# Opening of a two-layer decoder: two product tiles in one fixed order with the transposes, four k tiles apart

## The chip, the cores and the metric

The kernel runs on one core of a Trainium2 chip. The metric is the device time of one execution in microseconds (us), the median over several runs. The engines are TensorE (PE, matrix products and transposes), VectorE (DVE), ScalarE (ACT), GpSimd (POOL) and SyncE (SP). DMAs are issued from SP's queue and from ACT's; an issue on ACT's queue stands in the order of ACT's own work.

## What is computed

Two layers of a decoder with four parallel mixer branches, for 1024 prompt positions and 8 decoding rows. Each layer begins with a norm and one combined projection:

```
h = rms_norm(x, norm_g)
(a_b, a_c, a_h, a_gate, s_q, s_k, s_v, s_gate,
 c_u, c_v, c_gate, d_q, d_k, d_v, d_gate) = jnp.split(h @ w_in, SPLIT_POINTS, axis=-1)
z = a_c * a_h                                    # A: gated depthwise convolution of width 3
q = rope(s_q, pos); k = rope(s_k, pos); v = s_v  # B: sliding-window attention with sinks
vn = layer_norm(c_v, v_ln_g, v_ln_b)             # C: gating over chunks of 128 positions
dq = rope(d_q, pos); dk = rope(d_k, pos); dv = d_v   # D: three dilated attentions, joined by softmax
branches = stack([y_a * silu(a_gate), y_b * silu(s_gate), y_c * silu(c_gate), y_d * silu(d_gate)])
merged = sum(sigmoid(h @ w_merge) * (branches @ w_branch))
x = x + merged @ w_out
```

A last norm follows the second layer; caches and states are outputs too.

## The kernel before

**Layout.** The activations lie transposed: x^T in 8 k tiles of 128 rows by 1032 columns (8 decoding rows, then 1024 positions). Columns are taken in three chunks of 344 for the products and in three groups of 392, 384 and 256 for the start (`GROUPS`). Each fp32 product is made of three matmuls on a high and a low part (`mm_cols`, lines L178, L181, L182: h x wh, l x wh, h x wl). The parts of the weights come from ACT (hi, L154) and POOL (lo, L156), those of x^T from ACT (hi, L207) and DVE (lo, L209); for every fourth k tile ACT makes a scaled copy and POOL the low part (L213, L214). The norm's factor of a position, rtok, is applied to the results, so that products can start before the norm is known.

**The start (L251 to L272).** The input rows (xs: the decoding rows, xin: blocks of 128 positions) are loaded, 72 PE transposes (L259 for the 8 rows, L262 for a block) turn them into x^T by group and k tile, DVE copies each result from PSUM to xT (L264), and `split_x` makes both parts from that copy. Eight DMAs on ACT's queue store xT for the residual (L267), and nine squares on ACT (L272) sum up the squared rows.

**Then in each layer.** `rope_products` makes the key tile kB and the first query tile qB0, chunk by chunk, with ACT evicting each accumulator (L281). ACT's root (L325) and DVE's reciprocal (L326) give rtok. For the rotary factors rtok is spread over the partitions: DVE builds diagonal matrices dg (L332), PE multiplies them with ones (L333), ACT, DVE and POOL apply the result rr (L336 to L338). `rope` turns kB and qB0 (its shifted copies qs are DMAs on ACT's queue, L290). `tm_v` makes V for the window branch and the dilated branch, in blocks of 128 positions by 256 columns through `tm_group` (products L372, L375, L376; ACT evicts a block with its rtok at L391 and stores it at L393). A second query tile qB1 and then the gating branch's v, 384 columns wide, by the same lines L372 to L376, follow.

**Order.** Each engine runs its instructions in the order of its own queue. A scheduler sets that order from the program and from estimated times; `keep_in_program_order` pins an instruction to the place where it is written, and `issue_after` keeps everything issued inside it behind a given instruction. PSUM accumulators come from three pools: psA (three of one bank, `pacc`), psM (three of one bank, `pmisc`) and psS (one of two banks, `pscore`). A raw weight tile has two buffers, the split parts have four each.

**Further on.** The spatial weights wsp are loaded (L460) and transposed by PE (L465). `Decode.scores` transposes the decode queries on PE (L656). For the dilated groups (L890, L891, L906, L907) decode scores are issued ahead of a group's attention.

Of the kernel before, what the change touches and what calls it, by code (L numbers as in the profile page):

```python
# [7 lines left out]
F32 = mybir.dt.float32  # L8
F32R = mybir.dt.float32r
# [23 lines left out]
def kernel(ctx: ExitStack, tc: tile.TileContext, i, o, c):  # L33
# [65 lines left out]
    sp.dma_start(ident, c["ident"])  # L99
# [48 lines left out]

    def split_w(shape, dmas):
# [4 lines left out]
        act.activation(hi, raw, AF.Copy)  # L154
# [12 lines left out]
    def w_pair(l, c0, j):  # L167
# [4 lines left out]
        return r  # L172

# [30 lines left out]
    def split_x(l, k, cs, x, h, on_dve=True):  # L204

        g, hi, lo = gcol[:, l, k:k + 1], h[0][k][:, cs], h[1][k][:, cs]
        act.activation(hi, x, AF.Identity, scale=g)  # L207
        if on_dve:
            dve.scalar_tensor_tensor(lo, x, g, hi.bitcast(F32), op0=ALU.mult, op1=ALU.subtract)  # L209
# [22 lines left out]

    xs = slot("xs")[:NS, :DM]
    for q in range(2):
        fs = slice(q * DM // 2, (q + 1) * DM // 2)
        for n in range(3):
# [3 lines left out]
            if q == 0 and n == 0:  # L240
                sp.dma_start(xs, i["x_sample"].rearrange("b s d -> (b s) d"))
                sp.dma_start(gcol, i["norm_g"].rearrange("l (k p) -> p l k", p=P))
    w_first = [w_std(win_cols(0, S_K, P), KT)]
# [24 lines left out]
    sq0 = sm.tile([P, 9], F32, tag="sq0", name="sq0")  # L268
    junk = slot("junk")
    for n in range(9):  # L270
        src, M = (xin[n], P) if n < 8 else (xs, NS)
        act.activation(junk[:M, :DM], src[:M, :DM], AF.Square, accum_out=sq0[:M, n:n + 1])  # L272

    for l in range(2):
# [35 lines left out]
        w2 = w_first if l == 0 else [w_std(win_cols(l, S_K, P), KT)]  # L310
        w2.append(w_pair(l, S_Q, 0))
        kq = rope_products(w2, [slot("kB"), slot("qB0")])
# [14 lines left out]
        for n0, n1 in ((8, 9), (0, 4), (4, 8)):  # L327
            ps = pmisc()
            M = NS if n0 == 8 else P
            for n in range(n0, n1):  # L330
# [815 lines left out]
```

## Time and profile before

| | us |
|---|---|
| median of 3 runs | 2382.03 |
| lowest, highest | 2381.37, 2385.53 |
| profiled execution | 2387.34 |
| its span on the core | 2385.6 |
| PE busy within it | 2365.5 |
| DVE, ACT, POOL busy | 895.2, 687.4, 843.5 |

The times of single instructions come from the profiled execution. In its rows a line such as L178 is a line of the kernel above, `out<-in` are tile names, and xN joins N like instructions in a row; two instructions of an engine overlap by a part of their durations, so the distance between two starts is what one costs the engine. In the tables by windows PEclk is TensorE's granted clock as a share of its upper level (2.4 GHz; 0.50 is 1.2 GHz).

### The profile page before, as it was taken

The page shows a single profiled execution, that of the slowest core. Times are in us where ns is not written, and L with a number is a line of the kernel's source. Part 1 is how long each engine was busy: PE and PEld are TensorE (multiplying, and loading weights), DVE is VectorE, ACT ScalarE, POOL GpSimd, SP SyncE. Part 2 cuts the span into 40 slices and gives each one's busy share as a digit, 9 for nine tenths or more (in the row PEclk, how much of TensorE's full clock was granted, in tenths as well). Part 3 has the DMA queues.
Part 4 walks back from the last instruction along what each step waited for, and adds up shares of the span by engine and source line. Part 5 has one row for each costly group of instructions (what it writes and reads, how often), then busy time and mean ns, then how long its engine had stood idle before and what let it go on. Part 6 is the DMA issues. An engine that isn't in the chain of part 4 may idle for free.

```text
span 2385.6 us, 38754 instructions
## 1 busy us (share of the span) xinstructions
PE 2365.5 (99%) x15896; PEld 2305.1 (97%) x15896; DVE 895.2 (38%) x1938; ACT 687.4 (29%) x1522; POOL 843.5 (35%) x556
## 2 busy tenths in 40 slices
PE   7999999999999999999999999999999999999999
PEld 6999999999999999999999999999999999999999
DVE  4345466335312222324333455554452221213143
ACT  5133432223212222223322244323231221212243
POOL 3333234432223444434442322353322233444330
PEclk9999999999899999999999999999989999999999
DMA  7342423433322212224542423244442122222232
GB/s 237 98 123 79 119 69 109 132 102 106 100 71 88 77 55 97 64 70 123 150 146 72 145 72 98 69 151 113 111 126 67 58 91 66 98 67 62 75 99 101
DMA packets 295962, 235.82 MB, mean 99 GB/s; under 512 B 52756, under 2 KB 279696, under 8 KB 293416
## 3 DMA queue, kind: packets, MB, share of 16 engines
q1 hardware_dynamic: 267952, 206.25, 28.8%
q10 hardware_dynamic: 27832, 27.10, 4.1%
q8 instruction: 124, 2.03, 0.4%
q14 instruction: 54, 0.44, 0.1%
HBM read 192.35 MB, written 76.47 MB: 113 GB/s over the span
## 4 chain that ended last, share of the span: by engine, by line
PE 98%; DVE 1%; DMA 0%; ACT 0%; SPq 0%; issue 0%; ACTq 0%; DVEq 0%
PE acc L181 27%; PE acc L182 27%; PE acc L178 27%; PE acc L372 2%; PE acc L375 2%; PE acc L376 2%; PE sc L540 2%; PE ms L569 2%; PE ms L558 1%; PE ms L733 1%; PE ms L479 0%; PE ms L1042 0%; DMA wr<-in_w_in_dram 0%; DVE xT L264 0%; DVE h0l L209 0%; PE ms L333 0%
## 5 line engine op out<-in xcount | busy, mean ns | idle before, releaser
L156 POOL TENSOR_TENSOR wl<-wr,wh 128x384 fp32r<-128x384 f32 (+2 forms) x228 | 476.9, 2093 | 827.3 <-ACT wh L154 698.7
L181 PE MATMUL acc<-h1l,wh 128*128 128x344 f32 x1584 | 511.5, 323 | 0.0
L182 PE MATMUL acc<-h0h,wl 128*128 128x344 f32 x1584 | 510.4, 323 | 0.0
L178 PE MATMUL acc<-h0h,wh 128*128 128x344 f32 x1584 | 509.3, 322 | 0.9 <-DVE xT L264 0.9
L178 PE MATMUL acc<-h1h,wh 128*128 128x344 f32 x1584 | 510.2, 322 | 0.0
L182 PE MATMUL acc<-h1h,wl 128*128 128x344 f32 x1584 | 509.5, 322 | 0.0
L181 PE MATMUL acc<-h0l,wh 128*128 128x344 f32 x1584 | 508.9, 321 | 0.0
L154 ACT ACTIVATE wh<-wr 128x384 fp32r<-128x384 f32 (+2 forms) x228 | 205.2, 901 | 421.4 <-PE acc L181 393.6
L1005 DVE TENSOR_TENSOR th<-acc,rr 128x344 f32<-128x344 f32 x192 | 99.1, 516 | 553.5 <-PE acc L182 553.5
L181 PEld LDWEIGHTS acc<-h1l,wh 128*128 128x128 f32 x1584 | 299.9, 189 | 4.2 <-issue 3.6
L181 PEld LDWEIGHTS acc<-h0l,wh 128*128 128x128 f32 x1584 | 299.2, 189 | 3.9 <-issue 3.5
L182 PEld LDWEIGHTS acc<-h1h,wl 128*128 128x128 f32 x1584 | 299.7, 189 | 2.8 <-issue 2.3
L178 PEld LDWEIGHTS acc<-h0h,wh 128*128 128x128 f32 x1584 | 299.1, 189 | 2.8 <-issue 1.2
L182 PEld LDWEIGHTS acc<-h0h,wl 128*128 128x128 f32 x1584 | 298.6, 189 | 2.9 <-issue 2.3
L178 PEld LDWEIGHTS acc<-h1h,wh 128*128 128x128 f32 x1584 | 299.6, 189 | 1.4 <-issue 1.0
L1011 POOL TENSOR_TENSOR mg<-mg,th 128x344 f32<-128x344 f32 x144 | 134.0, 931 | 303.3 <-DVE th L1010 303.3
L1006 ACT ACTIVATE th<-th 128x344 f32<-128x344 f32 x192 | 94.3, 491 | 496.9 <-DVE th L1005 496.4
L178 PE MATMUL acc<-yh,wh 128*128 128x344 f32 x576 | 184.4, 321 | 0.0
L182 PE MATMUL acc<-yh,wl 128*128 128x344 f32 x576 | 184.3, 320 | 0.0
L181 PE MATMUL acc<-yl,wh 128*128 128x344 f32 x576 | 184.1, 320 | 0.0
L181 PE MATMUL acc<-ml,wh 128*128 128x344 f32 (+3 forms) x384 | 123.2, 321 | 0.0
L182 PE MATMUL acc<-mh,wl 128*128 128x344 f32 (+3 forms) x384 | 123.0, 321 | 0.0
(278 smaller groups left out, 3256.6 us busy)
## 6 DMA issues: line engine op xcount, KB each, us to landing
wr<-in_w_merge_dram SPq DMA_DIRECT2D x64, 512.0 KB
out_dram<-in_cache_dil_kv_dram SPq DMA_DIRECT2D x128, 255.9 KB
wr<-in_w_in_dram SPq DMA_DIRECT2D x60, 512.0 KB
y<-yscr SPq DMA_DIRECT2D x18, 516.0 KB
wr<-in_w_branch_dram SPq DMA_DIRECT2D x48, 192.0 KB
wr<-in_w_in_dram SPq DMA_DIRECT2D x32, 256.0 KB
wr<-in_w_out_dram SPq DMA_DIRECT2D x16, 512.0 KB
out_dram<-in_cache_dil_kv_dram SPq DMA_DIRECT2D x16, 511.0 KB
```

Of the source, the lines that this page charges most:

```text
L154: act.activation(hi, raw, AF.Copy)
L156: pool.tensor_tensor(lo, raw, hi.bitcast(F32), op=ALU.subtract)
L178: mm = pe.matmul(ps[:, :n], hi[:, k], xh[k][:, cs], start=(k == 0), stop=False)
L181: pe.matmul(ps[:, :n], hi[:, k], xl[k][:, cs], start=False, stop=False)
L182: pe.matmul(ps[:, :n], lo[:, k], xh[k][:, cs], start=False, stop=(k == kt - 1))
L372: mm = pe.matmul(ps[:M, :N], lh, hi[:, k % kk], start=(k == 0), stop=False)
L375: pe.matmul(ps[:M, :N], ll, hi[:, k % kk], start=False, stop=False)
L376: pe.matmul(ps[:M, :N], lh, lo[:, k % kk], start=False, stop=(k == KT - 1))
L540: pin(pe.matmul(ps[:, h, a * 256:a * 256 + u.nk], u.qs[h], u.ks[h], start=True, stop=True))
L1005: dve.tensor_tensor(t, pg[:, :CH], rr[:, cs], op=ALU.mult)
L1006: act.activation(t, t, AF.Tanh, scale=0.5)
L1011: pool.tensor_tensor(mg[m][:, cs], mg[m][:, cs], t, op=ALU.add)
```

## The change

- **Loads.** `ident`, `xs` and `gcol` are loaded from ACT's queue instead of SP's. The first two weight tiles are loaded in halves of four k tiles, between the halves of the input.
- **Dummy products.** 26 matmuls of a matrix of ones with itself into a bank nobody reads (`busy`): 18 at the start, 4 behind each of the first two turns.
- **Turns.** One k tile of one group is a turn. Its transposes go to psM, hi and lo are made from PSUM, lo always on DVE; xT is copied by ACT for even k and by DVE for odd k. Everything is pinned in the order written.
- **Two tiles in step.** Turns run two ahead of the first tile's products, and the second tile's products of a k tile come `LAG = 4` steps behind the first's. The accumulators of chunks 0 and 2 are both halves of psS's one tile, those of chunk 1 come from psA. Halves of weights are split at steps 0, 2, 3 and 6, squares stand at steps 7, 9, 12, 14, 17, 19 and behind the loop, the weights for the first V group are split at steps 18 and 22.
- **Behind the last eviction** of the opening, `issue_after` holds the stores of xT, the root for rtok and the first V group's evictions.
- **In both layers** the rr block and `rope` of kB and qB0 stand behind the first V group, the rr products, the transposes of wsp and of decode queries are pinned, wsp is loaded earlier, and the attention of the first two dilated groups is written ahead of their decode scores.

The diff, cut to its core:

```diff
     ident = cp.tile([P, P], F32, name="ident")
-    sp.dma_start(ident, c["ident"])
+    act.dma_start(ident, c["ident"])
...
+    idle = pacc()
+
+    def busy(n):
+        for _ in range(n):
+            in_order(pe.matmul(idle[:, :P], onesm, onesm, start=True, stop=True))
...
+                act.dma_start(xs, i["x_sample"].rearrange("b s d -> (b s) d"))
+                act.dma_start(gcol, i["norm_g"].rearrange("l (k p) -> p l k", p=P))
+        load_first(0, q)
+    for q in range(2):
+        load_first(1, q)
...
-    for n0, n1 in GROUPS:
+
+    def turn(n0, n1, k):
+
         off = NS if n0 == 0 else 0
         cs = slice(NS + n0 * P - off, NS + n1 * P)
         w = cs.stop - cs.start
-        for k in range(KT):
-            ks_ = slice(k * P, (k + 1) * P)
-            ps = pmisc() if k % 2 else pacc()
-            if off:
-                pe.transpose(ps[:, 0:NS], xs[:, ks_], ident[:NS, :NS])
-            for n in range(n0, n1):
-                c0 = off + (n - n0) * P
-                pe.transpose(ps[:, c0:c0 + P], xin[n][:, ks_], ident)
-            xt = xT0[k][:, cs]
-            dve.tensor_copy(xt, ps[:, :w])
-            split_x(0, k, cs, xt, (hh, hl), k % 4 != 1)
+        ks_ = slice(k * P, (k + 1) * P)
+        ps = pmisc()
+        if off:
+            in_order(pe.transpose(ps[:, 0:NS], xs[:, ks_], ident[:NS, :NS]))
+        for n in range(n0, n1):
+            c0 = off + (n - n0) * P
+            in_order(pe.transpose(ps[:, c0:c0 + P], xin[n][:, ks_], ident))
+        xt = xT0[k][:, cs]
+        if k % 2:
+            in_order(dve.tensor_copy(xt, ps[:, :w]))
+        split_x(0, k, cs, ps[:, :w], (hh, hl))
+        if k % 2 == 0:
+            in_order(act.activation(xt, ps[:, :w], AF.Copy))
...
+    def split_first(a, q):
+        ks_ = slice(4 * q, 4 * q + 4)
+        raw = w_first[a][:, ks_]
+        hi, lo = [t[:, ks_] for t in wf[a]]
+        in_order(act.activation(hi, raw, AF.Copy))
+        pool.tensor_tensor(lo, raw, hi.bitcast(F32), op=ALU.subtract)
+
+    accs = []
+
+    def first_products(a, s):
+
+        c, k = s // KT, s % KT
+        if k == 0 and a == 0:
+            if c == 1:
+                accs.append([pacc(), pacc()])
+            else:
+                two = pscore()
+                accs.append([two[:, 0], two[:, 1]])
+        ps, cs = accs[c][a][:, :CH], slice(c * CH, (c + 1) * CH)
+        hi, lo = [t[:, k] for t in wf[a]]
+        mm = in_order(pe.matmul(ps, hi, hh[k][:, cs], start=(k == 0), stop=False))
+        if s == 0:
+            mark(mm)
+        in_order(pe.matmul(ps, hi, hl[k][:, cs], start=False, stop=False))
+        in_order(pe.matmul(ps, lo, hh[k][:, cs], start=False, stop=(k == KT - 1)))
+        if k == KT - 1:
+            done.append(lambda: in_order(act.activation(kq0[a][:, cs], ps, AF.Copy)))
...
+    LAG = 4
+    squares = (7, 9, 12, 14, 17, 19)
+    for s in range(3 * KT + LAG):
+        if s == 0:
+            for t in turns[:2]:
+                turn(*t[0], t[1])
+                busy(4)
+            split_first(0, 0)
+        if s in (2, 3, 6):
+            split_first(*{2: (0, 1), 3: (1, 0), 6: (1, 1)}[s])
+        if s + 2 < len(turns):
+            turn(*turns[s + 2][0], turns[s + 2][1])
+        while done:
+            done.pop(0)()
+        if s in (18, 22):
+            w_v.append(tm_weights(0, V_FIRST, 4, 4 * len(w_v)))
+        if s in squares:
+            square(squares.index(s))
+        if s < 3 * KT:
+            first_products(0, s)
+        if s >= LAG:
+            first_products(1, s - LAG)
+    for n in range(6, 9):
+        square(n)
+    while done:
+        last = done.pop(0)()
+    opening[0] = False
+    behind_opening = ExitStack()
+    behind_opening.enter_context(tc.issue_after(last.ins))
     for k in range(KT):
         act.dma_start(xres[0][k], xT0[k])
...
+        if l == 0:
+            kq = kq0
+        else:
+            kq = rope_products([w_std(win_cols(l, S_K, P), KT), w_pair(l, S_Q, 0)], [slot("kB"), slot("qB0")])
...
+        tm_v(V_FIRST, 0, w_v if l == 0 else None)
+        behind_opening.close()
+
+        for n0, n1 in ((8, 9), (0, 4), (4, 8)):
+            ps = pmisc()
+            M = NS if n0 == 8 else P
+            for n in range(n0, n1):
+                dg = sm.tile([P, P], F32, tag="dg", name="dg", bufs=2)
+                dve.tensor_scalar(dg[:M, :M], ident[:M, :M], rtok[:M, n:n + 1], None, op0=ALU.mult)
+                tc.keep_in_program_order(pe.matmul(ps[:, (n - n0) * P:(n - n0) * P + M], onesm[:M], dg[:M, :M],
+                                                   start=True, stop=True))
...
         kB, qB = rope(kq[0]), [rope(kq[1])]
-        tm_v([(S_V, P), (D_V, P)], 0)
...
-                pe.transpose(ps[:, g * P:(g + 1) * P], wsp[:, g0 + g], ident)
+                tc.keep_in_program_order(pe.transpose(ps[:, g * P:(g + 1) * P], wsp[:, g0 + g], ident))
...
-                pe.transpose(ps[:NS, :P], q, ident)
+                tc.keep_in_program_order(pe.transpose(ps[:NS, :P], q, ident))
...
+        attention()
         decD.scores(0, dqs[0], dks[0])
-        attention()
...
```

**First place: PE, step 8 of the opening.** Here the second tile's product of k = 4 in chunk 0 (accumulator `sc`, input h0h_135) stands. Before, the first products stood behind all transposes of the first two groups:

```order
L262 MATMUL ms<-ident,xin_120 128x128
L262 MATMUL ms<-ident,xin_122 128x128
L178 MATMUL acc<-h0h_128,wh 128x344
L181 MATMUL acc<-h0l_136,wh 128x344
L182 MATMUL acc<-h0h_128,wl 128x344
L178 MATMUL acc<-h0h_129,wh 128x344
L181 MATMUL acc<-h0l_137,wh 128x344
L182 MATMUL acc<-h0h_129,wl 128x344
```

Now, with what each waits for:

```order
L302 MATMUL ms<-ident,xin_117 128x128 [waits PE_49]
L302 MATMUL ms<-ident,xin_119 128x128
L302 MATMUL ms<-ident,xin_121 128x128
L345 MATMUL acc<-h0h_131,wh 128x344 [waits Activation_49]
L348 MATMUL acc<-h0l_139,wh 128x344 [waits DVE_49]
L349 MATMUL acc<-h0h_131,wl 128x344
L345 MATMUL sc<-h0h_135,wh 128x344 [waits Activation_49]
L348 MATMUL sc<-h0l_143,wh 128x344
L349 MATMUL sc<-h0h_135,wl 128x344 [waits Pool_49]
```

A turn's transposes, the first tile's product of chunk 1 (`acc`) and the second tile's of chunk 0 (`sc`) now alternate; the last of these waits for ACT.

**Second place: ACT, from the kB eviction to the V evictions.** Before, the table load and the root stood ahead of the last evictions, and the stores of xT far ahead:

```order
L272 ACTIVATE junk,sq_340<-xs 8x1024
L325 ACT_TABLE_LOAD
L325 ACTIVATE rtok<-sq_340,epst 128x8
L154 ACTIVATE wh<-wr 128x1024
L281 ACTIVATE kB<-acc 128x344
L325 ACTIVATE rtok<-sq_340,epst 8x1
L154 ACTIVATE wh<-wr 128x768
L281 ACTIVATE qB_359<-acc 128x344
L336 ACTIVATE rr<-ms 128x8
```

Now, with the waits:

```order
L162 ACTIVATE wh<-wr 128x768 [waits DMAHW5_49,PE_49,Pool_49]
L351 ACTIVATE qB_176<-sc 128x344 [waits PE_49]
L383 DMA xres_94<-xT_0_147 128x1032
L383 DMA xres_94<-xT_1_148 128x1032
L383 DMA xres_94<-xT_2_149 128x1032 [waits DMAHW1_49]
L383 DMA xres_94<-xT_3_150 128x1032 [waits DMAHW2_49]
L383 DMA xres_94<-xT_4_151 128x1032
L383 DMA xres_94<-xT_5_152 128x1032
L383 DMA xres_94<-xT_6_153 128x1032 [waits DMAHW6_49]
L383 DMA xres_94<-xT_7_154 128x1032 [waits DMAHW7_49]
L437 ACT_TABLE_LOAD
L437 ACTIVATE rtok<-sq_155,epst 128x8
```

Eight issues of stores, the table load and the root now stand behind the last eviction; three V evictions (L483) follow them.

**Third place: PE, the first dilated group.** Before, the decode query's transpose (dqs) stood with the transposes of the convolution's state and ahead of attention transposes (s):

```order
L780 MATMUL ms<-ident,stt 128x16
L781 MATMUL ms<-ident,z 8x128
L782 MATMUL ms<-ident,z 2x128
L656 MATMUL ms<-ident,dqs_3172 8x128
L558 MATMUL ms<-ident,s 128x128 x4
```

Now:

```order
L201 MATMUL acc<-h0l_144,wh 128x344
L202 MATMUL acc<-h0h_136,wl 128x344
L676 MATMUL ms<-pt,v_3397 64x128 x8
L763 MATMUL ms<-ident,dqs_3190 8x128
L198 MATMUL acc<-h0h_137,wh 128x344
```

It now stands behind the group's products with V (L676).

## Rows read from the trace of the kernel before

**Rows 1.** Page, busy time: engine, busy us, share of the span, instructions.

```profile
PE 2365.5 (99%) x15896; PEld 2305.1 (97%) x15896; DVE 895.2 (38%) x1938; ACT 687.4 (29%) x1522; POOL 843.5 (35%) x556
```

**Rows 2.** Waits of PE: line, what for, us in total, times, longest.

```profile
PE acc L259 <- DMA xs<-in_x_sample_dram: 4.8, 1, 4.8
PE ms L333 <- DVE dg L332: 3.8, 3, 1.5
```

**Rows 3.** Windows: length, busy of PE, PEld, DVE, ACT, POOL, PEclk, DMA share, GB/s.

```profile
0.00:25.00 25.00, 15.63 (x66) 11.13 (x66) 12.27 (x23) 11.08 (x19) 6.00 (x13) 0.86 0.88 243
...
50.00:75.00 25.00, 22.16 (x173) 21.92 (x172) 10.51 (x16) 6.43 (x15) 9.92 (x6) 0.93 0.43 122
```

**Rows 4.** Timeline of PE: start, us, engine, line, operation, [idle before <-releaser].

```profile
27.23 0.40 PE L178 MATMUL acc<-h0h,wh 128*128 128x344 f32 x1 [0.94 <-DVE xT L264]
...
50.42 0.28 PE L372 MATMUL acc<-wh,h0h 128*128 128x256 f32 x1
50.54 0.28 PE L375 MATMUL acc<-wh,h0l 128*128 128x256 f32 x1
...
53.62 0.36 PE L333 MATMUL ms<-dg,onesm 8*128 8x8 f32 x2 [1.39 <-DVE dg L332]
55.44 0.46 PE L333 MATMUL ms<-dg,onesm 128*128 128x128 f32 x2 [1.45 <-DVE dg L332]
...
93.99 0.34 PE L372 MATMUL acc<-wh,h0h 128*128 128x384 f32 x1
```

**Rows 5.** Timeline of ACT and of its DMA queue (ACTq), same columns.

```profile
9.48 0.62 ACT L207 ACTIVATE h0h<-xT,gcol 128x392 fp32r<-128x392 f32 x1 [1.87 <-DVE xT L264]
...
22.34 2.12 ACT L207 ACTIVATE h0h<-xT,gcol 128x384 fp32r<-128x384 f32 x4
...
24.45 0.35 ACTq L267 DMA_DIRECT2D xres<-xT  x1
...
28.98 1.99 ACT L207 ACTIVATE h0h<-xT,gcol 128x256 fp32r<-128x256 f32 x4
...
38.28 0.44 ACT L281 ACTIVATE kB<-acc 128x344 f32<-128x344 f32 x1
38.62 1.05 ACT L272 ACTIVATE junk<-xin 128x1024 f32<-128x1024 f32 x1
...
48.41 1.28 ACT L325 ACT_TABLE_LOAD   x1
49.71 0.30 ACT L325 ACTIVATE rtok<-sq,epst 128x8 f32<-128x8 f32 x1
...
51.38 0.83 ACT L154 ACTIVATE wh<-wr 128x768 fp32r<-128x768 f32 x1
...
54.10 2.54 ACTq L290 DMA_DIRECT2D qs<-kB  x4
...
65.23 0.47 ACT L391 ACTIVATE vn<-acc,rtok 128x256 f32<-128x256 f32 x1 [0.92 <-PE acc L376]
65.73 4.70 ACTq L393 DMA_DIRECT2D vscr<-vn  x1
```

**Rows 6.** Timeline of DVE.

```profile
8.88 0.57 DVE L264 COPY xT<-acc 128x392 f32<-128x392 f32 x1 [7.92 <-PE acc L262]
10.13 0.63 DVE L209 SCALAR_TENSOR_TENSOR h0l<-xT,gcol,h0h 128x392 fp32r<-128x392 f32 x1 [0.69 <-ACT h0h L207]
...
50.04 0.20 DVE L326 RECIPROCAL rtok<-rtok 128x8 f32<-128x8 f32 x1 [12.01 <-ACT rtok L325]
```

**Rows 7.** Timeline of POOL.

```profile
13.78 2.34 POOL L156 TENSOR_TENSOR wl<-wr,wh 128x1024 fp32r<-128x1024 f32 x1 [0.22 <-ACT wh L154]
```

**Rows 8.** Timeline of PE, transposes of the spatial weights, at full clock.

```profile
169.34 0.82 PE L465 MATMUL ms<-ident,wsp 128*128 128x128 f32 x6
```

**Rows 9.** Timeline of PE in layer 1.

```profile
1234.32 0.49 PE L333 MATMUL ms<-dg,onesm 128*128 128x128 f32 x2 [0.91 <-DVE dg L332]
```

**Rows 10.** Timeline of DVE at the first dilated group.

```profile
339.81 2.59 DVE L795 SCALAR_TENSOR_TENSOR yA<-s,cw,yA 128x8 f32<-128x8 f32 x2
```

More of the change, by code (lines that the diff above doesn't have):

```diff
@@ L172, in w_pair, with tm_weights @@
         return r
+    def tm_weights(l, srcs, kk, k0):
+        dmas, c0 = [], 0
+        for col, n in srcs:
+            src = i["w_in"][l, k0 * P:(k0 + kk) * P, col:col + n].rearrange("(k p) m -> p k m", p=P)
+            dmas.append((lambda t, c0=c0, n=n: t[:, :, c0:c0 + n], src))
+            c0 += n
+        r = split_w([P, kk, c0], dmas)
+        copy_piece()
+        return r
+    V_FIRST = [(S_V, P), (D_V, P)]
     def mm_cols(ps, w, kt, xh, xl, cs, first):
@@ L231, in load_x, with load_first @@
             xin.append(xb)
+    idle = pacc()
+    def busy(n):
+        for _ in range(n):
+            in_order(pe.matmul(idle[:, :P], onesm, onesm, start=True, stop=True))
     xs = slot("xs")[:NS, :DM]
+    w_first = [wp.tile([P, KT, P], F32, tag="wr", name="wr", bufs=2) for _ in range(2)]
+    def load_first(t, q):
+        ks_ = slice(4 * q, 4 * q + 4)
+        if t == 0:
+            sp.dma_start(w_first[0][:, ks_], win_cols(0, S_K, P)[:, ks_])
+            return
+        for h in range(2):
+            sp.dma_start(w_first[1][:, ks_, h * 64:(h + 1) * 64], win_cols(0, S_Q + 192 * h, 64)[:, ks_])
     for q in range(2):
@@ new lines, in turn @@
+        ps = pmisc()
[10 more added lines that the diff above has]
+            in_order(act.activation(xt, ps[:, :w], AF.Copy))
+    sq0 = sm.tile([P, 9], F32, tag="sq0", name="sq0")
@@ new lines, with square @@
+    junk = slot("junk")
+    def square(n):
+        src, M = (xin[n], P) if n < 8 else (xs, NS)
+        return in_order(act.activation(junk[:M, :DM], src[:M, :DM], AF.Square, accum_out=sq0[:M, n:n + 1]))
+    busy(18)
+    kq0 = [slot("kB"), slot("qB0")]
+    turns = [(g, k) for g in GROUPS for k in range(KT)]
+    wf = [[wp.tile([P, KT, P], F32R, tag=t, name=t, bufs=4) for t in ("wh", "wl")] for _ in range(2)]
+    w_v = []
+    done = []
+    def split_first(a, q):
+        ks_ = slice(4 * q, 4 * q + 4)
+        raw = w_first[a][:, ks_]
+        hi, lo = [t[:, ks_] for t in wf[a]]
+        in_order(act.activation(hi, raw, AF.Copy))
+        pool.tensor_tensor(lo, raw, hi.bitcast(F32), op=ALU.subtract)
@@ L326 @@
             dve.reciprocal(rtok[:M, ps_], rtok[:M, ps_])
[L327 to L330, printed above, removed]
-                dg = sm.tile([P, P], F32, tag="dg", name="dg", bufs=2)
-                dve.tensor_scalar(dg[:M, :M], ident[:M, :M], rtok[:M, n:n + 1], None, op0=ALU.mult)
-                pe.matmul(ps[:, (n - n0) * P:(n - n0) * P + M], onesm[:M], dg[:M, :M], start=True, stop=True)
-            cs = slice(0, NS) if n0 == 8 else slice(NS + n0 * P, NS + n1 * P)
-            w = cs.stop - cs.start
-            act.activation(rr[:, cs], ps[:, :w], AF.Copy)
-            dve.tensor_tensor(cosT[:, cs], cosT[:, cs], rr[:, cs], op=ALU.mult)
-            pool.tensor_tensor(sinT[:, cs], sinT[:, cs], rr[:, cs], op=ALU.mult)
         cw = sm.tile([P, 3, 3], F32, tag="cw", name="cw")
@@ L443 @@
         bsps = [lngb[:, 6 * P:7 * P], lngb[:, 7 * P:8 * P], wsps[:, 6 * P:7 * P]]
+        load(wsp, i["w_spatial"][l].rearrange("g t s -> t g s"), 2)
         for h in range(2):
@@ L905 @@
         rows()
+        attention()
         decD.scores(1, dqs[1], dks[1])
-        attention()
         out_a(1)
```

45 lines of the change are left out of this document (17 added, 28 removed).

## The prediction

> **What bounds the kernel now.** I read the page's engine table first. TensorE (PE) is busy 99% of the span [rows 1], so an edit pays only by what it takes out of PE's idle time, out of a stretch at half clock, or out of PE's own work. The waits of PE come next [rows 2]: 4.8 us at the start for the sample rows' load, which no edit here removes; 3.8 us in three waits for the diagonal matrices that DVE builds at L332. The table by windows says where it lies [rows 3]: PE is busy 15.63 of the first 25 us, and 22.16 of those from 50 to 75 at a mean granted clock of 0.93, which is 0.07 x 25 = 1.75 us lost to stretches at the lower level (1.2 GHz). From 75 on PE is full, so everything is decided before the first 384-column product of the third group (L372) at 93.99. I call this instant the milestone; what moves it moves the end.
>
> The timeline of PE gives four stations [rows 4]: first product at 27.23, last key/query product just before 50.42, where the V products begin, waits of 1.39 and 1.45 us for L332, and the milestone at 93.99. The 144 products of the first two tiles and the few transposes among them take 23.19 us, so one product costs 0.158, that is 22.75 for all. A 256-column V product costs 0.118 (50.42 to 50.54). From 50.42 to 93.99 are 43.57 us; less both waits and the clock's 1.75 it is 38.98 of steady work.
>
> **The start of the products.** Product 0 now needs one turn instead of all transposes. Before, the first copy of x^T began at 8.88 and the first hi at 9.48 [rows 5, 6]; hi now reads PSUM without that copy, so I start it at S = 8.5 (8 to 9.5). Behind it stand a half split of the weights (0.83 for 768 columns, so an estimate of 0.55 for 512, [rows 5]) and, for the third matmul, POOL's half (2.34 / 2 = 1.2, [rows 7]): the first product is near 9.8 and flows from about 11, 16 us earlier. The dummy products fill time in which PE has nothing else. Their kind is that of L333, of which two took 0.46 [rows 4], so at most 0.23 each, twice that at half clock: 18 of them are 4 to 8 us, about as long as x takes to land, and the other eight 0 to 1.8 us beside the hi that PE waits for. I take 0 and let S reach 9.5.
>
> That is no gain of 16 us, since the transposes now lie among the products. 64 of the 72 do. Six warm transposes in a row took 0.82 [rows 8], so 0.12 each by that row once the last one's tail is taken off: 64 x 0.12 = 7.7. Each turn is also a chain through ACT and DVE.
>
> **ACT's chain, pair by pair.** DVE's lo begins 0.65 after its hi and takes 0.63 (9.48, 10.13, [rows 5, 6]). The order of ACT puts the copy of the even k tile behind that lo, and the next hi behind DVE's copy (0.57): 0.65 + 0.63 + 0.57 + 0.05 of hand-over = 1.90, and 0.53 for that hi (four took 2.12) is 2.43 a pair. For the last group, of 256 columns, hi is 0.50 (four took 1.99), and the pair shrinks by the width to about 1.93. Twelve pairs are 8 x 2.43 + 4 x 1.93 = 27.2; up to the last pair's first hi 25.2. Into this order are put: four half splits (4 x 0.55 = 2.2), six squares (6 x 1.1 = 6.6, by 1.05 and the read of the sum behind it), three evictions (3 x 0.38 = 1.1, by 0.44 less the overlap), one split of V weights (1.05, like a square of the same 1024 columns) [rows 5]. Sum 25.2 + 2.2 + 6.6 + 1.1 + 1.05 = 36.1. So ACT reaches the last pair at 8.5 + 36.1 = 44.6 if PE never holds it up.
>
> PE does. The chunk 0 accumulators of both tiles are one tile now, so the second tile's product of k = 4 waits until the first tile's accumulator has been evicted. PE's own order and ACT's (the first two places shown with the diff) put that eviction behind a split, two hi, a copy, a square, another hi and its copy. From hi of k = 7 on that is 0.53 + 0.53 + 2.43 + 1.05 + 1.28 + 0.44 = 6.3 on ACT, while PE has 9 products and 3 transposes (1.8) and one hi-lo latency (1.28): a hole of about 3 us, in which ACT later waits for the next turn's transposes. With POOL's lo, waited for twice, I put 3 us of PE's making into the chain (0 to 6): 47.6. Then lo (0.5) and what PE still has: in order 23 key/query products (3.6) and 54 V products (6.4). **Last key/query product: 47.6 + 0.5 + 10.0 = 58.1** against 50.42 before, but with 58 of the V products (6.8) done ahead of it.
>
> **From there to the milestone.** PE has 14 V products left (1.65 us), then the fourth V block needs the accumulator of the first, which needs rtok. ACT's order behind the last product is: a 768 split whose buffer that product frees (0.83), the eviction (0.35), eight issues of the x^T stores (8 x 0.35 = 2.8), the table load (1.28), the root (0.30, and the same for the decoding rows' root, beside which DVE's reciprocal runs, 0.20), the V eviction (0.47) [rows 5, 6]: 6.4 us, less 1.65 of cover, a stall of 4.8. Before, the stores' issues lay between hi's in the open stretch, and the load was covered by products. Behind such a stall the clock has fallen before (1.75). Milestone: 58.1 + (38.98 - 6.84) + 4.8 + 1.75 = 96.8, which is **+2.8 us** on 93.99. The 1.39 and 1.45 waits for L332 are gone, this stall stands in their place.
>
> The Trainium skill, page "ScalarE: Activation LUTs", section "What ACT_TABLE_LOAD costs", speaks against putting the load on this path: it counts 1.28 us and a drain of 1.38, 2.66 for a switch. By that the stall would be 6.2 and the time 1.4 later. The row agrees with the 1.28 and not with the drain: the load ran 48.41 to 49.69 and the root began at 49.71 [rows 5]. I stay with the row.
>
> **Later edits.** In layer 1 the dg products stand behind the V group, so PE's wait of 0.91 there [rows 9] should go: -0.9. The spatial weights' load goes earlier and its transposes are pinned: cover is the full PE around them, nothing. The rotary sums with their eight issues on ACT's queue (four took 2.54, [rows 5]) stand behind V's evictions instead of ahead of them; who reads their result comes after the second query tile's 72 products (11.4), so nothing. Decode transposes pinned, and the first two dilated groups' attention ahead of decode scores (the third place shown with the diff): one q transpose moves some 40 rows, so 24 products (3.8 us) that stood between the scores and their masks no longer do, while DVE may stand 2.59 us in L795 behind POOL [rows 10]. Between no loss and 1.5 us a layer; I take +0.6 for both, near the low end, since the products around it can still be put ahead. Sum: 2.8 - 0.9 + 0.6 = **+2.5**.
>
> The profiled execution (2387.34) lies 5.3 above the median of its kernel; its stages are used as differences, so the forecast is 2382.03 + 2.5 = 2384.5.
>
> **The rivals.**
> *PE sets the pace (faster).* If ACT keeps up, because turns run two ahead, the stream is PE's sum: 11 + 22.75 + 6.84 + 7.7 + 1 = 49.3, the milestone 49.3 + 32.1 + 4.8 + 1.75 = 88.0, with the 0.9 of layer 1 -6.9: 2375. With the eviction's hole of 3 us left in, 2378. For it: ACT's sum has 12 x 0.65 of mere waiting for DVE. Against: the order forces that wait. Without the stall at the fourth block and its half clock as well, 2369 (the least likely).
> *The queue of ACT blocks at the stores (slower).* Four of the eight issues wait for an earlier DMA, and all of ACT's work behind them waits too, above all the root. Before, an issue on ACT's queue stood 4.70 us in such a wait (65.73, [rows 5]). One such wait here is +4.7: 2389. The cover of 1.65 is used up already, so a wait adds in full, and from 2.3 us on it decides (2.5 + 2.3 = 4.8). Against: by 59 us the loads of the start have long landed.
> *The attention's order costs in both layers (slower).* +1.5 twice instead of 0.6: 2387.
> *It does not do what it says.* The pinned order holds by construction; but the gain is only moved: transposes into the stream, V products ahead, waits of 2.84 for one of 4.8. That is my forecast.
>
> **How the numbers follow.** About 0.2% (4.8 us) is what a measurement can tell from no change: 2377.3 to 2386.8. My sum, with 0 to 6 us for PE's holds and 8 to 9.5 for S, gives 2381 to 2388: chance 0.47, most of it within the bound. PE's pace 0.27, of which 0.05 ends within the bound (2378). Blocked stores 0.15, attention 0.11, half of it within the bound. Faster 0.24, same 0.48, slower 0.28. The range reaches to 2374 for PE's pace and to 2391 for a blocked issue on top of my sum's upper half; below and above lie 0.1 each.
>
> **What would show it.** The first product near 10 to 11; PE's waits list naming ACT's kB eviction with about 3 us near 25; the last 344-column product of the first group near 58 with V products among the last ones; the fourth V block waiting 4 to 6 us for ACT's V eviction, and half clock behind it; the milestone at 96 to 98; no wait for L332 in either layer. I am wrong if the first products run without holes (PE's pace), if ACT's hi follow one another closer than 2.4 us a pair, or if the milestone is right and the end is not, which puts the error on the attention.

## The result, and the profile of the changed kernel

The changed kernel takes 2411.93 us (median of 4, 2410.96 to 2415.04) against 2383.78 for the kernel before, measured beside it: a ratio of 1.0111 (95% interval 1.0095 to 1.0128), 28 us slower. The forecast was +2.5 and its range ended at 2391. Line numbers below are those of the changed kernel: L227 and L229 make hi and lo, L329 and L330 split the first weights, L345, L348 and L349 are the products of the first two tiles, L351 evicts them, L383 stores xT, L437 is the root, L464, L467 and L468 are the V products, L483 their eviction. In the waits s are the attention's scores, wsT the masked spatial weights, qB the second query tile, vcs the decoding rows' V, qr a decoding query, dqp the rotated query of a dilated group.

The page's table of engines, which answers to [rows 1] (busy us, share of the span, instructions):

```profile
span 2413.3 us, 38855 instructions
PE 2377.1 (99%) x15948; PEld 2315.3 (96%) x15948; DVE 901.7 (37%) x1932; ACT 690.4 (29%) x1530; POOL 844.6 (35%) x552
```

PE's idle time is 2413.3 - 2377.1 = 36.2 us instead of 20.1, and its busy time is 11.6 longer. The first entries of PE's list of waits (total, times, longest; [rows 2] is that of before):

```profile
PE acc L464 <- ACT vn L483: 9.5, 1, 9.5
PE ms L665 <- ACT s L697: 3.7, 2, 1.8
PE sc L345 <- ACT wh L329: 3.4, 1, 3.4
PE ms L586 <- POOL wsT L574: 3.3, 1, 3.3
PE acc L464 <- ACT qB L392: 3.1, 1, 3.1
PE sc L345 <- ACT kB L351: 2.7, 1, 2.7
PE ms L774 <- DVE qr L765: 2.0, 3, 0.8
```

No wait for the diagonal matrices is left, in neither layer. In their place stand a stall of 9.5 at the fourth V block, and four kinds of waits that the whole list of before doesn't have, for s, wsT, qB and qr. The four together are 12.1 us, and they lie behind the opening.

The table by windows of PE's first 107 us, of 5 us within them and of what follows (columns as in [rows 3]), cut at the milestone, the first 384-column product:

```profile
0.00:106.98 106.98, 88.80 (x572) 82.40 (x573) 25.70 (x51) 44.85 (x87) 20.41 (x21) 0.90 0.54 157
15.00:20.00 5.00, 4.53 (x16) 3.37 (x17) 1.82 (x3) 2.00 (x5) 1.43 (x2) 0.50 1.00 397
106.98:213.00 106.02, 102.75 (x744) 97.80 (x744) 50.24 (x96) 25.14 (x48) 44.81 (x24) 1.00 0.40 118
1213.00:1313.00 100.00, 96.86 (x657) 95.67 (x657) 31.39 (x40) 23.24 (x43) 33.06 (x17) 0.97 0.41 118
```

and of the kernel before, cut at its own milestone:

```profile
0.00:93.99 93.99, 79.99 (x522) 74.39 (x523) 42.47 (x64) 43.15 (x80) 34.81 (x28) 0.95 0.62 185
```

These give the ledger of the 27.7 us between the two spans. **Up to the milestone: +13.0.** Idle time grows from 14.0 to 18.2 (+4.2), and busy time from 80.0 to 88.8 (+8.8). The 26 dummy products alone are 8.1 of that busy time (line, engine, operation, form, records | busy us, mean ns | idle before):

```profile
L258 PE MATMUL acc<-onesm 128*128 128x128 f32 x52 | 8.1, 323 | 1.1 <-POOL epst L109 1.1
```

They fill time in which PE has nothing else, so they hide idle time rather than add delay: idle and dummy together are 26.3 us instead of 14.0. By the trace's clock records PE was busy for 15.8 us at the lower level (0.50) instead of 8.3, which costs 3.7 more; its other work is about 3.0 shorter. The dummy products didn't keep the clock up for the first products: PE then waited 3.40 for the split weights, and the granted clock stood at the lower level from 14.9 to 21.8.

**Behind it: +14.7.** Idle there is 36.2 - 18.2 = 18.0 instead of 20.1 - 14.0 = 6.1 (+11.9); the other 2.8 is busy time. Half of that is clock (33.5 us of it at the lower level instead of 30.7, 1.4 lost); what the other half is stays open. So the larger half of the loss lies where the forecast had -0.3.

**The opening on ACT.** ACT's timeline at the start and behind the last key/query product (start, duration; ACTq is the issuing of DMAs in ACT's order; [rows 5] is that of before):

```profile
10.70 1.28 ACT L227 ACT_TABLE_LOAD   x1 [10.70 <-DMA gcol<-in_norm_g_dram]
11.99 0.59 ACT L227 ACTIVATE h0h<-ms,gcol 128x392 fp32r<-128x392 f32 x1
...
51.34 0.47 ACT L227 ACTIVATE h0h<-ms,gcol 128x256 fp32r<-128x256 f32 x1
...
62.73 0.84 ACTq L383 DMA_DIRECT2D xres<-xT  x2
63.37 0.44 ACT L351 ACTIVATE qB<-sc 128x344 f32<-128x344 f32 x1
63.61 7.75 ACTq L383 DMA_DIRECT2D xres<-xT  x6
71.39 1.28 ACT L437 ACT_TABLE_LOAD   x1 [7.59 <-DMA xres<-xT]
72.69 0.48 ACT L437 ACTIVATE rtok<-sq,epst 128x8 f32<-128x8 f32 x2
73.26 0.84 ACT L483 ACTIVATE vn<-acc,rtok 128x256 f32<-128x256 f32 x2
```

The first hi begins at 11.99, 1.28 of table load behind the norm factors gcol, which are now loaded from ACT's queue. The eight stores of xT occupy ACT's queue from 62.73 to 71.36, and the root, the V eviction and with them PE stand behind. The DMA engines were full meanwhile (columns as in [rows 3]):

```profile
64.00:66.00 2.00, 0.34 (x3) 0.14 (x2) 0.00 (x0) 0.00 (x0) 1.35 (x1) 1.00 0.99 394
```

PE's stations ([rows 4] before):

```profile
14.90 0.66 PE L345 MATMUL sc<-h0h,wh 128*128 128x344 f32 x1 [3.40 <-ACT wh L329]
31.73 0.45 PE L345 MATMUL sc<-h0h,wh 128*128 128x344 f32 x1 [2.73 <-ACT kB L351]
62.37 0.32 PE L349 MATMUL sc<-h0h,wl 128*128 128x344 f32 x1
73.79 0.58 PE L464 MATMUL acc<-wh,h0h 128*128 128x256 f32 x1 [9.45 <-ACT vn L483]
106.98 0.34 PE L464 MATMUL acc<-wh,h0h 128*128 128x384 f32 x1
```

**Behind the opening.** ACT, POOL and PE around the masked spatial weights wsT; L494 stores V rows to an output:

```profile
185.77 1.28 ACTq L494 DMA_DIRECT2D out_dram<-vn  x1
...
190.19 0.34 ACTq L494 DMA_DIRECT2D out_dram<-vn  x1
190.57 0.47 ACT L483 ACTIVATE vcs<-acc,rtok 8x256 f32<-8x256 f32 x1 [6.98 <-DMA out_dram<-vn]
190.94 1.04 ACT L162 ACTIVATE wh<-wr 128x1024 fp32r<-128x1024 f32 x1
...
192.06 4.69 POOL L164 TENSOR_TENSOR wl<-wr,wh 128x1024 fp32r<-128x1024 f32 x2 [24.02 <-ACT wh L162]
196.71 0.86 POOL L574 TENSOR_SCALAR_AFFINE_SELECT wsT<-wsT 128x768 f32<-128x768 f32 x1
...
197.62 1.97 PE L586 MATMUL ms<-wsT,cv 128*64 128x128 f32 x32 [3.27 <-POOL wsT L574]
```

A chain: the issues of two stores hold ACT's queue from 185.77 to 190.53, of which 3.1 us pass between the first and the second, ACT's eviction and split come after them, POOL's two splits after that, the mask behind them, and PE waits 3.27. The same pattern stands in layer 1, where a rope copy's issue blocks ACT for 6.40, 1.9 us behind the issue of a cache copy on SP's queue:

```profile
1268.98 0.62 SPq L93 DMA_DIRECT2D out_dram<-in_cache_dil_kv_dram  x1
1270.88 6.40 ACTq L401 DMA_DIRECT2D qs<-kB  x1
...
1284.29 0.60 ACT L512 ACTIVATE rr<-ms 128x512 f32<-128x512 f32 x1 [11.67 <-DMA qs<-kB]
1284.79 0.80 ACT L392 ACTIVATE qB<-acc 128x344 f32<-128x344 f32 x2
...
1285.29 0.69 PE L464 MATMUL acc<-wh,h1h 128*128 128x384 f32 x1 [3.13 <-ACT qB L392]
```

### The profile page after: what moved, and what is told of

It reads as the page before. It is cut to its first block, busy times and chain, and to the rows that moved or that the text cites. A ratio compares the mean times of both kernels' runs of the same rounds, so it can differ in the third digit from the quotient of the medians.

```text
span 2413.3 us, 38855 instructions
## 1 busy us (share of the span) xinstructions
PE 2377.1 (99%) x15948; PEld 2315.3 (96%) x15948; DVE 901.7 (37%) x1932; ACT 690.4 (29%) x1530; POOL 844.6 (35%) x552
## 4 chain that ended last, share of the span: by engine, by line
PE 91%; DMA 3%; DVE 2%; ACT 1%; ACTq 1%; issue 1%; POOL 1%; SPq 0%; DVEq 0%; POOLq 0%
PE acc L198 26%; PE acc L201 26%; PE acc L202 26%; PE acc L464 2%; PE acc L467 2%; PE acc L468 2%; PE sc L647 2%; PE ms L676 2%; PE ms L665 1%; PE ms L840 1%; DMA vscr<-vn 1%; DMA wr<-in_w_in_dram 1%; PE ms L586 0%; POOL qs L402 0%; ACTq L401 0%
## 5 line engine op out<-in xcount | busy, mean ns | idle before, releaser
L198 PE MATMUL acc<-h0h,wh 128*128 128x344 f32 x1536 | 495.5, 323 | 0.0
L202 PE MATMUL acc<-h0h,wl 128*128 128x344 f32 x1536 | 494.5, 322 | 0.0
L201 PE MATMUL acc<-h0l,wh 128*128 128x344 f32 x1536 | 494.2, 322 | 0.0
L201 PEld LDWEIGHTS acc<-h0l,wh 128*128 128x128 f32 x1536 | 290.2, 189 | 4.5 <-issue 4.2
L202 PEld LDWEIGHTS acc<-h0h,wl 128*128 128x128 f32 x1536 | 290.3, 189 | 1.9 <-issue 1.5
L198 PEld LDWEIGHTS acc<-h0h,wh 128*128 128x128 f32 x1536 | 289.8, 189 | 1.7 <-issue 1.3
```

Of the source, the lines that this page charges most:

```text
L198: mm = pe.matmul(ps[:, :n], hi[:, k], xh[k][:, cs], start=(k == 0), stop=False)
L201: pe.matmul(ps[:, :n], hi[:, k], xl[k][:, cs], start=False, stop=False)
L202: pe.matmul(ps[:, :n], lo[:, k], xh[k][:, cs], start=False, stop=(k == kt - 1))
```

## First experiments: one suspect undone at a time

Four suspects: the row of stores on ACT's queue, the small loads moved to ACT's queue, the attention's place ahead of the decode scores, and the rope's issues behind the V group. Each is taken out of the changed kernel alone. The ratio of each run is to the kernel before, beside it on the chip.

**The stores freed.** They are written where `issue_after` has closed, and the scheduler spreads them.

```diff
-    for k in range(KT):
-        act.dma_start(xres[0][k], xT0[k])
...
         behind_opening.close()
+        if l == 0:
+            for k in range(KT):
+                act.dma_start(xres[0][k], xT0[k])
```

> The eight stores of x^T are no longer held behind the opening's last eviction; each goes on ACT's queue as its k tile is ready, among the last group's turns. Theory A (a row of eight issues of 516 KB costs ACT the time of the transfers, 8.66 us instead of the 2.8 of the prediction, and the root for rtok stands behind it): the fourth V block waits 1 to 4 us instead of 9.5, the first 384-column product comes at 98 to 101 instead of 107, the time falls by 6 to 10 us. Theory B (the late start of hi, 11.99 instead of about 8, carries the loss, and ACT's chain would end as late without the stores): the first 384-column product moves by less than 3 us, and so does the time.

Measured: 2406.75, ratio 1.0090 (1.0069 to 1.0112). The stores now lie between 42.69 and 53.00. PE's waits:

```profile
PE sc L648 <- DVE dqp L411: 5.2, 3, 4.3
PE ms L666 <- ACT s L698: 4.2, 3, 1.8
PE ms L587 <- POOL wsT L575: 3.6, 1, 3.6
...
PE acc L462 <- ACT vn L481: 1.9, 1, 1.9
```

The stall at the fourth V block falls from 9.45 to 1.94, and the milestone from 106.98 to 96.28. Of these 10.7 us less than half reaches the end, and the intervals overlap. A wait of 4.3 for dqp appears later. The row of stores is the cause of the stall; it isn't the cause of the whole loss.

**The small loads back on SP's queue** (`act.dma_start` to `sp.dma_start` for `ident`, `xs` and `gcol`).

> The three small loads (identity, decoding rows, norm weights) go back to SP's queue, as before the change. Theory A: the norm weights land near 6.5 instead of 10.7, the first hi runs at 8 to 9 instead of 12.0, the first product at 10 to 11.5 instead of 14.9; the wait of the fourth V block stays at about 9 us, the time falls by 3 to 4 us. Theory B: by 8 us or more, since the whole chain of the opening moves with it.

Measured: 2410.63, 1.0108 (1.0091 to 1.0125). The first hi begins at 8.49 and the first product at 11.78, 3.1 to 3.5 us earlier, and the milestone at 105.82, 1.2 earlier. The rest goes into a wait of 2.3 for DVE's lo, because a small DVE instruction (nsink) waits in front of it for a late load.

**Attention back behind the decode scores** (two pairs of lines exchanged).

> The attention of the first two dilated groups stands behind their decode scores again, in both layers. If the new order costs what the waits show (1.8 and 0.7 us in layer 0, 1.8 and 1.2 in layer 1, and half clock behind them for a while): 4 to 8 us faster than the changed kernel, with no wait for L697 left. If those waits only take the place of others: within 1.5 us of it.

Measured: 2408.53, 1.0104 (1.0084 to 1.0124); the two waits of 1.8 for L697 are gone, and the time is not separated from the changed kernel's.

**rr and rope of layer 1 ahead of the V group again.**

> In layer 1 alone the rr block and the rotation of kB and qB0 stand ahead of the first V group again. If the eight shifted copies on ACT's queue hold qB1's evictions there (PE waits 3.1 us at 1282, then runs at half clock): that wait is gone, one of about 0.9 for L507 comes back, and the time falls by 3 to 6 us. If the prediction was right that these issues cost nothing: 1 us slower.

Measured: 2417.47, 1.0135 (1.0120 to 1.0150). The wait for qB is gone, but a wait of 4.0 for vcs (`L483`) stands in its place, and PE waits 0.9 for dg again. The block of ACT's queue moved on: a V store's issue stands 5.80 there, behind a cache copy again. So rope's place isn't the reason for it.

## The two halves apart

> The new opening alone: rr block, rotation, spatial weights, decode transposes and the order of attention and decode scores as in the kernel before, in both layers. Theory A (the opening loses what the first 384-column product shows, 13 us, and the later edits lose the rest): 11 to 16 us over the kernel before, no wait for L697 and none of about 3 us for the spatial weights. Theory C (the opening alone shifts the queues for the whole run, and the later waits come from that): 20 us or more over it, with the later waits still there.

The opening alone (all that comes behind it as before): 2424.98, 1.0157 (1.0141 to 1.0172). PE's waits:

```profile
PE ms L445 <- DVE dg L444: 11.6, 3, 9.4
PE acc L198 <- ACT vcs L495: 5.8, 2, 5.1
PE ms L585 <- POOL wsT L573: 3.8, 1, 3.8
```

> The kernel before with the later edits alone: rr and rotation behind the first V group in both layers, pinned products and transposes, earlier spatial weights, attention ahead of decode scores in the first two dilated groups. Theory A: 8 to 14 us over the kernel before, with the waits for L697 (about 1.8 us in each layer) and one for qB1's evictions in layer 1. Theory C: within 3 us of it.

The later edits alone, on the kernel before: 2389.06, 1.0014 (1.0005 to 1.0024). Their milestone is 91.51, 2.5 earlier than before: with the rr block behind the V group nothing waits for L332 any more. They lose it again at the attention (4.5 us in three waits for s). So the opening makes the loss, and the later edits save part of it. The rr block's new place is the likely one, which no run tries by itself: without it the stall stands at dg, with 9.4, as it stood at the V eviction with it. And the waits for wsT and vcs, far behind the opening, come with the opening.

**Mending what was found.** The opening alone and the whole changed kernel, each with the stores freed and the small loads on SP's queue:

> The new opening alone, with the three small loads on SP's queue and the stores of x^T not held behind the last eviction. By theory A both mends add to it: stall of the fourth V block below 2 us, first product near 11, first 384-column product at 94 to 97; the time within 4 us of the kernel before, on either side. By theory C, 8 us or more over it.

> The changed kernel with the same two mends and all later edits kept. Theory A: 9 to 12 us under the changed kernel, 12 to 17 over the kernel before, so that the later edits show alone by the distance to the run with the opening alone. If the two mends overlap (the late start is hidden in the stall): 5 to 7 us under the changed kernel.

2418.18, 1.0131 (1.0116 to 1.0146), and 2400.83, 1.0061 (1.0043 to 1.0080). The second has its milestone at 97.18 and a V stall of 1.8, and is still 15 us slower than the kernel before. The wait for wsT is there in both (3.8 and 3.2). Something in the opening disturbs what comes 80 us and 1100 us later.

## What the opening moved without naming it

The code has it. Copies of the caches (DRAM to DRAM, up to 511 KB) are put on SP's queue a piece at a time, one with each weight load, and the helper leaves out the first eight loads: `if pieces and nload[0] > 8`. The new opening loads its first two weight tiles without calling that helper. So the count starts two loads late, and **the cache copies stand later in SP's queue**: before at places 37, 42, 43, 44, 57, 59, 61, now at 41, 42, 55, 57, 59, 62, 65 (the second alone keeps its place).

The trace has two ways in which they hold ACT. The program's DMAs signal through eight semaphores which SP's and ACT's queues share, so that a DMA on ACT's queue also has to wait for an earlier one that used the same semaphore. The second V store shows it: its semaphore was last used by a 508 KB copy that SP issued at 175.71, that copy's last landing is recorded at 190.16, and the store is issued at 190.19.

The rope copy at 1270.88 is another matter: its own semaphore's last DMA had landed by 1257.50. It stood while the 508 KB copy of 1268.98, on another semaphore, was under way; that one landed from 1276.72 to 1277.52, and the issue ended at 1277.28. In the seventeen traces twelve issues on ACT's queue stood over 3 us. Each began 1.4 to 4.3 us behind the issue of such a copy, with its own semaphore free, and eight ended 0.2 to 0.3 us ahead of the copy's last landing, the others earlier. One of the twelve is in the kernel before: the 4.70 at 65.73 [rows 5].

```profile
62.96 0.74 SPq L93 DMA_DIRECT2D out_dram<-in_cache_swa_kv_dram  x1
```

Not every issue during a copy stands (three just ahead of 1270.88 took 0.33 to 0.46), and what makes one stand no run here shows.

In the changed kernel a count that starts at 2 puts the first fourteen copies back to their places:

```diff
-    nload = [0]
+    nload = [2]
```

> The changed kernel with one number changed: the counter that holds back the cache copies starts at 2, since the new opening no longer counts its first two weight loads. Every cache copy on SP's queue stands again where it stood before the change (places 37, 42, 43, 44, 57 of that queue instead of 41, 42, 55, 57, 59). Theory D (the shift put two 508 KB copies among ACT's V stores, which wait for them by a shared DMA semaphore, and ACT's later work behind them: the masked spatial weights at 197, the evictions in layer 1): the wait of 3.3 us for the spatial weights and the one of 3.1 us in layer 1 are gone or below 1 us, the time falls by 6 to 12 us; the fourth V block still waits 8 to 10 us. Theory C' (any change of the opening puts the queues out of step, whatever the copies): within 3 us of the changed kernel.

> The new opening alone with the copies at their old places. Theory D: 15 to 25 us under the run with the opening alone (2425), no wait for the spatial weights, none of 5 us for the decoding rows' V in layer 1. Theory C': within 4 us of 2425.

The changed kernel so mended: 2408.60, 1.0086 (1.0059 to 1.0113). The opening alone so mended: 2409.27, 1.0081 (1.0052 to 1.0110), against 1.0157 (1.0141 to 1.0172) without it: 18 us by the ratios, clearly apart. In the changed kernel the gain is 3.3 by the medians and 6 by the ratios, and the intervals overlap; its trace shows PE behind the milestone and at the start of layer 1:

```profile
106.32:213.00 106.68, 106.68 (x771) 101.45 (x770) 52.84 (x110) 27.38 (x58) 45.37 (x24) 1.00 0.40 117
...
1213.00:1313.00 100.00, 100.00 (x688) 99.09 (x687) 32.10 (x43) 22.80 (x42) 32.49 (x17) 1.00 0.40 117
```

Full, where the changed kernel had 3.3 and 3.1 us of idle time and a clock of 0.97. The waits for wsT, vcs and qB are gone in both kernels. The same rope copy that stood 6.40 us is issued in 0.56:

```profile
1269.80 0.56 ACTq L401 DMA_DIRECT2D qs<-kB  x1
```

That the copies' place causes these waits is shown, since the edit changes nothing else. What they cost is shown for the opening alone; in the changed kernel it isn't clear of the noise.

**All mends together.** Stores freed, small loads on SP, attention back in both groups, copies back; and the same with nsink held behind the last lo and each eviction written ahead of the next turn:

```diff
-        if s + 2 < len(turns):
-            turn(*turns[s + 2][0], turns[s + 2][1])
         while done:
             done.pop(0)()
+        if s + 2 < len(turns):
+            turn(*turns[s + 2][0], turns[s + 2][1])
```

> The changed kernel with four mends: small loads on SP's queue, stores of x^T not held, copies at their old places, attention behind the decode scores. If they add (11 for the first two as measured, 3.4 for the attention, 6 to 12 for the copies): 2386 to 2392, that is 0 to 6 us over the kernel before. If they overlap: 2394 to 2399.

> As the run before it, and two small moves in the opening: the scaled sinks on DVE are held behind the last lo (they waited 4.4 us for their load with two lo behind them, 3.0 us of PE), and an eviction stands ahead of the next turn's hi and copy (2.8 us of PE for kB). If PE's own stream then sets the pace: 4 to 6 us under the run before, 2380 to 2387, the first 384-column product at 88 to 91. If ACT's chain does, as the prediction had it: within 2 us of the run before.

2393.09, 1.0016 (0.9998 to 1.0035), milestone 95.27; and 2390.32, 1.0008 (0.9991 to 1.0024), milestone 92.21. The hole behind kB's eviction shrinks from 2.73 to 1.5 in the first and to 1.1 in the second. With all of it undone or mended about 2 of the 28 us remain, and the interval includes zero. What each mend is worth by itself depends on the others, since a wait that goes uncovers the next.

## Does the opening bring anything?

The best of the opening (all mends, attention ahead of the scores only in the second dilated group) against the later edits alone with the same attention on the kernel before:

> The mended opening (small loads on SP's queue, stores not held, copies at their old places, sinks held behind the last lo, evictions ahead of the next turn) with the later edits, the attention ahead of the decode scores only in the second dilated group. If the opening is worth what PE no longer waits for at the start (the first 384-column product at 92 against 94): 2380 to 2385, 2 to 6 us under the kernel before, and 1 to 4 under the run with the later edits alone. If its gain is used up: level with the later edits alone.

> The kernel before with the later edits alone, the attention ahead of the decode scores only in the second dilated group. The first 384-column product at 91 to 92 as in the run with all later edits, the waits for L697's counterpart gone in the first group: 2 to 4 us under that run, so 0 to 3 us under the kernel before.

2387.98, 1.0006 (0.9996 to 1.0017), milestone 91.92; and **2382.87, 0.9983 (0.9974 to 0.9991)**, milestone 91.42. The second beats the kernel before by about 4 us. Its interval lies apart from that of the first, and from that of the later edits with both groups moved (1.0005 to 1.0024). Two things follow. The first group's attention ahead of its scores costs about 6 us over both layers (7 by the ratios) on the kernel before; in the changed kernel no run separates it from nothing. And the interleaved opening, mended as far as I could, brings its milestone to the same place as the old one and is about 5 us worse at the end. In the first of the two, PE's waits begin with

```profile
PE sc L651 <- DVE dqp L413: 5.3, 2, 4.5
```

of which 4.5 us stand in layer 0's second dilated group, where the attention's scores wait for their rotated query; the second has no such wait there. The same wait was 4.3 with the stores freed alone. What moves it stays open.

**The row of stores by itself**, in the kernel before: the eight stores held behind the last square and pinned in a row.

```diff
+    with tc.issue_after(last.ins):
+        for k in range(KT):
+            tc.keep_in_program_order(act.dma_start(xres[0][k], xT0[k]))
```

> The kernel before with one edit: its eight stores of x^T stand in a row behind the last square, ahead of the root for rtok. Theory A (a row of them takes ACT the time of the transfers, about 8.7 us): the waits for the diagonal matrices in layer 0 grow from 2.8 us to 7 to 10, the time by 4 to 9 us. The prediction's price (8 x 0.35 = 2.8): the waits grow by under 2 us, the time by under 2.

Measured: 2386.18, 1.0003 (0.9990 to 1.0016). ACT's timeline:

```profile
46.75 1.65 ACTq L273 DMA_DIRECT2D xres<-xT  x3
...
48.43 6.40 ACTq L273 DMA_DIRECT2D xres<-xT  x5
54.87 0.46 ACT L282 ACTIVATE kB<-acc 128x344 f32<-128x344 f32 x1 [6.98 <-DMA xres<-xT]
```

The row costs ACT's queue 8.1 us here too, so the price is the row's, not the new opening's. But PE's waits for dg stay at 3.2 (before 3.8) and the time doesn't move: PE had V products left to run, and the scheduler put the first dg product behind more of them (57.71 instead of 53.62). In the changed kernel only some 14 V products were left behind the last key/query product, which end near 64.3.

## Why the prediction was wrong, step by step

- **What bounds the kernel: right, but cut short.** "From 75 on PE is full, so everything is decided before" the milestone was true of the kernel before and was carried over to the changed one. This step failed first: 14.7 of the 27.7 us arose behind the milestone. Later runs say the same: with the stores held in the kernel before, the milestone came 2.2 later (96.19) and the end didn't, and the last two kernels with the same attention have their milestones within 0.5 and end 5 us apart.
- **The start, S: mis-sized.** Taken as 8.5 (8 to 9.5), it was 11.99. The three small loads' change of queue was never priced; gcol landed at 10.70 instead of 6.32. First product 14.90 for 9.8: 3.5 of it is S, and 1.6 more came because ACT's order has the second turn's hi ahead of the split of the weights. Run with the loads on SP's queue, S was 8.49, and the milestone moved by 1.2 only.
- **The dummy products: right size from a misread row.** "Two took 0.46, so at most 0.23 each" takes the two records of one product for two products; the 26 dummies have 52 records (L258). One costs 0.33 in a row. 18 of them took 6.0, within "4 to 8" because that allowed for half clock, while the granted clock stood at its upper level.
- **ACT's chain: right.** From the first hi to that of the last pair 39.1 were forecast (36.1 and 3 for PE's holds); 51.34 - 11.99 = 39.35 were measured. The hole behind kB's eviction, "about 3 us", was 2.73. The rival that PE sets the pace was wrong for this order; with evictions and nsink moved, the milestone still fell by 3.1 (95.27 to 92.21), so part of the chain was holds that the order made.
- **Last key/query product:** 58.1 forecast, 62.37 measured. 3.5 of the 4.3 come from S.
- **The stall at the fourth V block: right place, half the size.** 4.8 forecast, 9.45 measured. The failing term is "eight issues x 0.35 = 2.8": 0.35 was an issue with others of ACT's work around it, and the row took 8.66. The table load (1.28, root 1.30 behind its start) and the eviction held. The drain of 1.38 that the Trainium skill's page "ScalarE: Activation LUTs", section "What ACT_TABLE_LOAD costs", counts behind the load didn't show here either: the load began at 71.39 and the root at 72.69. The rival "the queue of ACT blocks at the stores" named the place, but as one wait of 4.7 on an earlier DMA; it was the row itself, in which the two issues at 65.66 and 66.91 took 1.22 and 1.35 with no DMA to wait for. Its row of 4.70 was misread as well: that issue's semaphore had been free since 60.54, and it stood while a cache copy was under way. So the coupling that was missing from the forecast stood in a row of before.
- **The milestone:** forecast 96.8, measured 106.98. Of the 10.2 missing, 4.3 lie ahead of the last product, 4.65 in the stall, and the rest, about 1.2, behind it: the granted clock stood at its lower level until 79.8, which on 6.0 us of busy PE is 3.0 lost for the 1.75 forecast. With the stores freed it was 96.28, within 0.6 of the forecast, by luck: the late S was still in it, and the stall was 1.9 instead of 4.8.
- **rr behind the V group: right.** No wait for dg in either layer; -2.5 at the milestone of the later edits alone.
- **Rope's issues "nothing": the size not refuted, the reason incomplete.** It asked who reads their result, not what stands behind them on ACT's queue: in the changed kernel that was qB1's evictions, and PE waited 3.13. That wait went away with the cache copies, and undoing the move didn't pay.
- **The attention: right sign, too small where it could be measured.** +0.6 for both layers; on the kernel before the first group alone cost about 6. In the changed kernel its waits (1.8 a layer) are seen, its cost isn't separated from nothing.
- **What was missing altogether: the cache copies.** The prediction counted what each listed edit issues and every queue that it is moved past. It didn't ask which loads no longer pass through a helper that counts them. The diff shows the new loads, not the helper; the places in SP's queue would have shown it. The idle time behind the milestone is about half this and half the attention: of 11.9 us more, 6.4 are the waits for wsT and qB, which the copies' old places removed, and most of the rest those for s and qr (5.7), which the attention's old place removed.

## To carry to other kernels

Where an edit takes a DMA out of a helper that counts or paces others, compare the places of all DMAs in the queues before and after, not only of those that the diff names. Price a row of large DMA issues on a computing engine's queue by its transfer time, and look for what on that engine, and on PE, stands behind it. Run the halves of a combined change apart: here a small gain lay in a part of the later edits, and was buried under the attention's order and the opening.

## What the runs showed of the hardware that I had not expected

- **A row of large issues runs near the pace of its transfers.** Over the changed kernel's eight stores the issue times (minimum, median, maximum in ns, and the first and last start) are

```profile
L383 ACTq DMA_DIRECT2D xres<-xT x8: 361/1210/1688, 62.7 to 70.0; - x8
```

  At 516 KB (528,384 bytes) each, 4.23 MB in 8.63 us are about 490 GB/s, while the DMA engines were full (share 0.99 at 394 GB/s from 64 to 66); in the kernel before with its stores held, 8.1 us give 520. Spread among other work, in the run with the stores freed, seven of the eight issues took 0.33 to 0.47 and one 1.25.
- **A small load from the second queue landed later.** gcol, issued at 1.88 on ACT's queue, landed at 10.70; issued from SP's queue, at 6.32 in the kernel before and at 6.13 in the changed kernel with the small loads back.
- **An issue on one queue can stand for a DMA of the other.** 6.40 us for a rope copy on ACT's queue while SP's 508 KB copy of 1268.98 was under way, without a semaphore in common; with SP's copies elsewhere the rope copy took 0.56.
